# A decoder layer on one core: the merge by halves of the tokens, the first half inside the recurrent stage's stream of products

## The chip, the core and the metric

The kernel runs on one core of a Trainium2 chip. A core has five engines with a queue of instructions each: TensorE (PE, matrix products; its weight loads, PEld, overlap them), VectorE (DVE), ScalarE (ACT), GpSimd (POOL) and SyncE (SP). Each works through its own queue in order, and an instruction that waits holds up all that stand behind it on that engine. Products are summed in PSUM, eight banks of 128 x 512 float32; everything else lives in SBUF. DMAs are issued from the queues of SP, ACT and POOL. The metric is the time of one launch in microseconds (us) on the device; the median of the runs is what counts.

## What is computed

One decoder layer over 512 tokens of width 1024, in float32. Two branches run on the same normalised rows, attention (`y_a`) and a recurrence (`y_b`), are raised to full width, gated, added, and projected; a norm and a feed-forward part follow.

```python
y_a = _diff_branch(p_q, p_k, p_v, ...)
y_b = _rwkv_branch(p_rwkv, ...)          # a scan over the 512 tokens
merged = (jax.nn.sigmoid(p_ga) * (y_a @ w_up_a[l])
          + jax.nn.sigmoid(p_gb) * (y_b @ w_up_b[l]))
mix = merged @ w_out[l]
h = _layer_norm(DEEPNORM_ALPHA * h + mix, ln1_g[l], ln1_b[l])
ffn = (jax.nn.silu(h @ ffn_w_gate[l]) * (h @ ffn_w_up[l])) @ ffn_w_down[l]
h = _layer_norm(DEEPNORM_ALPHA * h + ffn, ln2_g[l], ln2_b[l])
```

`w_up_b` is 512 x 1024, `w_out` 1024 x 1024, the feed-forward width 2816.

## The kernel before

Every large product is done in split precision: a float32 operand is held as a rounded part (h) and a remainder (l), and `three` (L79) issues three matmuls, h·h, h·l and l·h. A piece of weights is 128 x 1024 floats (512 KB). SP loads it into one of two buffers `w_raw`, ACT casts it to h (L75), DVE subtracts to get l (L76), and both land in rotating tiles `w_h` and `w_l` (three of each). `split_psum` (L116) does the same for activations.

The kernel has three parts. First entry norm, attention, and the projections. Second the recurrent stage (L757 to L985), whose instructions are written out in an order that the program works out itself: generators yield the costs they expect on PE, DVE and ACT, and a small planner (L936 to L983) keeps a clock for each engine and takes the first task that is ready. The order of the list is the priority. Ahead stand the recurrence's steps: `chains`, `posts` (finishing of 128 tokens each: norm over heads, gain, gate), `applies`, `rwkv_solve`, `pres`, `mids`, and `yb_split`, which splits the finished `y_b` into h and l. Behind stand the fill tasks: `stream(gates)` and `ups`, the up-projection of `y_a`, both through `stream` (L787), which prefetches two pieces ahead. The list `fill` names them, for a rule that gives them a least share of PE. Each engine gets its instructions in that order; instructions of what follows the stage may be put between them by the framework where it finds an engine free.

Post `tb` ends with L655 to L661: for the first three blocks of 128 tokens y goes out to DRAM on POOL's queue (`y_d`) and `yb_split` loads it back; the last block stays in SBUF (`y_last`).

Third, L988 on: the merge. For each of four column groups j, `group_a` (L84) does the up-projection of `y_b` over all 512 tokens (24 matmuls of 512 columns); `gated` (L782) multiplies with the stored gate `thb`, DVE adds the attention branch's `tha`, ACT and DVE split the sum into `mg` (L1009 to L1012); then one piece of `w_out` serves the output products of columns 0 to 511 for all four blocks of 128 rows (L1014 to L1023). After that come the output products of columns 512 to 1023 (`out_proj`, L1038), block of rows by block of rows; each ends with the residual, the norm and a store of `h1`; `to_h2` (L1062) transposes a block of normalised rows into `h2`, the operand of the feed-forward products. The first gate and up group of the feed-forward part is done by halves of the tokens (L1100 to L1112), with `to_h2(2)` and `to_h2(3)` in its order. Outside the recurrent stage the framework orders instructions by their readiness and by place in the program.

## Time and profile before

| | us |
|---|---|
| median of 3 runs | 890.8 |
| the runs | 895.94, 890.8, 890.51 |
| the profiled execution | 890.32 |
| its span, first to last instruction | 888.6 |
| PE busy in the span | 834.4 |
| mean granted clock | 0.979 |

All working below is against the one profiled execution. A line of the profile that begins with a time is an instruction (or several like it) in order of time: start, duration, engine, line, operation, what it writes and reads, the shape, and in brackets how long the engine stood idle before it and what released it. A line that begins with a line number is a group: count, busy time and mean duration in ns of one, then idle time before. In the table of stretches each engine has its busy time and in brackets its instructions; the granted clock (1.00 is full speed) follows them. Two matmuls overlap, so their pace is the distance of their starts, not their duration.

### The profile page before, as it was taken

Reading aid. Unit: us, or ns where it says so; the run is one execution under the profiler, and the core shown is the slowest. Engines: PE = TensorE matmul, PEld = TensorE weight load, DVE = VectorE, ACT = ScalarE, POOL = GpSimd, SP = SyncE. Lnnn points to the kernel's source line nnn. Section 1 sums busy time; section 2 is a strip of 40 time slices with the busy share of each in tenths; the row PEclk is TensorE's granted clock in tenths of the full one; section 3 lists DMA queues with packets and bytes.
Section 4 is the critical chain, followed back from the end, with each engine's and each line's share of the span. In section 5 each row is a group of like instructions: output and inputs, shape, how many; then the busy total and the mean of one; then the engine's idle time right before and its main releaser. Section 6 shows DMA issues by size and latency. Waiting matters only on the chain. (4 is left out here: it accounts for less than half of the span.)

```text
span 888.6 us, 13458 instructions
## 1 busy us (share of the span) xinstructions
PE 834.4 (94%) x5486; PEld 684.7 (77%) x5486; DVE 457.2 (51%) x821; ACT 329.1 (37%) x572; POOL 82.5 (9%) x126
## 2 busy tenths in 40 slices
PE   3999999989799998988799999999999999999996
PEld 2877977878678776766577898888888888888885
DVE  6767494564648345636456954334434433324227
ACT  4566485736442344532124122222232223211210
POOL 5012010012230001201000100000000000000003
PEclk9999999998799999999799999999999999999999
DMA  6561422233234712134374444333333332222322
GB/s 224 152 215 53 127 60 83 72 96 72 54 90 142 169 48 96 61 107 155 101 268 141 142 178 137 105 102 96 95 94 95 95 95 95 95 96 71 120 71 96
DMA packets 75596, 99.15 MB, mean 112 GB/s; under 512 B 8431, under 2 KB 58154, under 8 KB 75534
## 3 DMA queue, kind: packets, MB, share of 16 engines
q1 hardware_dynamic: 70206, 80.72, 30.2%
q10 hardware_dynamic: 3488, 11.54, 3.5%
q0 software_dynamic: 1840, 6.03, 2.2%
q8 instruction: 43, 0.70, 0.3%
q14 instruction: 19, 0.16, 0.0%
HBM read 84.90 MB, written 14.69 MB: 112 GB/s over the span
## 5 line engine op out<-in xcount | busy, mean ns | idle before, releaser
L80 PE MATMUL mm_ps<-act_h,w_h 128*128 128x512 f32 x624 | 252.1, 404 | 1.0 <-ACT w_h L75 1.0
L82 PE MATMUL mm_ps<-act_h,w_l 128*128 128x512 f32 x624 | 245.7, 394 | 0.5 <-DVE w_l L76 0.5
L81 PE MATMUL mm_ps<-act_l,w_h 128*128 128x512 f32 x624 | 245.4, 393 | 0.0
L76 DVE TENSOR_TENSOR w_l<-w_raw,w_h 128x1024 fp32r<-128x1024 f32 x84 | 102.7, 1224 | 151.1 <-ACT w_h L75 150.9
L75 ACT CAST w_h<-w_raw 128x1024 fp32r<-128x1024 f32 x84 | 88.3, 1051 | 201.4 <-PE acc_ps L82 81.2
L82 PEld LDWEIGHTS mm_ps<-act_h,w_l 128*128 128x128 f32 x624 | 118.4, 190 | 25.3 <-DVE w_l L76 1.0
L80 PEld LDWEIGHTS mm_ps<-act_h,w_h 128*128 128x128 f32 x624 | 118.3, 190 | 25.1 <-ACT w_h L75 1.4
L81 PEld LDWEIGHTS mm_ps<-act_l,w_h 128*128 128x128 f32 x624 | 118.4, 190 | 21.7
L100 POOL TENSOR_TENSOR rs<-ve,mhalf 128x1 f32<-128x1 f32 (+1 forms) x32 | 29.4, 920 | 511.7 <-DVE ve L98 436.9
L82 PE MATMUL acc_ps<-w_h,hid_l 128*128 128x512 f32 (+1 forms) x198 | 73.4, 371 | 0.0
L81 PE MATMUL acc_ps<-w_l,hid_h 128*128 128x512 f32 (+1 forms) x198 | 73.3, 370 | 0.0
L80 PE MATMUL acc_ps<-w_h,hid_h 128*128 128x512 f32 (+1 forms) x198 | 73.2, 370 | 0.0
L804 DVE TENSOR_TENSOR w_l<-w_raw,w_h 128x1024 fp32r<-128x1024 f32 x32 | 39.0, 1222 | 37.1 <-ACT w_h L803 37.1
L80 PEld LDWEIGHTS acc_ps<-w_h,hid_h 128*128 128x128 f32 x198 | 37.3, 188 | 7.1
L82 PEld LDWEIGHTS acc_ps<-w_h,hid_l 128*128 128x128 f32 x198 | 37.3, 188 | 7.0
L81 PEld LDWEIGHTS acc_ps<-w_l,hid_h 128*128 128x128 f32 x198 | 37.2, 188 | 6.9
L803 ACT CAST w_h<-w_raw 128x1024 fp32r<-128x1024 f32 x32 | 33.4, 1047 | 16.2 <-PE mm_ps L81 13.8
L1092 ACT CAST hid_h<-sl 128x512 fp32r<-128x512 f32 x22 | 13.6, 617 | 54.0 <-DVE sl L1090 54.0
L1090 DVE SCALAR_TENSOR_TENSOR sl<-sl,mm_ps 128x512 f32<-128x512 f32 x20 | 13.8, 688 | 33.1 <-PE mm_ps L82 33.1
L1087 DVE SCALAR_TENSOR_TENSOR sl<-sl,mm_ps 128x512 f32<-128x512 f32 x20 | 13.7, 685 | 33.0 <-ACT sl L1086 33.0
L81 PE MATMUL acc_ps<-wo_l,mg_h 128*128 128x512 f32 x64 | 25.2, 394 | 2.1 <-DVE wo_l L1018 2.1
L1086 ACT ACTIVATE sl<-mm_ps 128x512 f32<-128x512 f32 x20 | 11.8, 592 | 39.9 <-PE mm_ps L82 39.9
(266 smaller groups left out, 1242.9 us busy)
## 6 DMA issues: line engine op xcount, KB each, us to landing
w_raw<-in_w_in SPq DMA_DIRECT2D x42, 512.0 KB
w_raw<-in_ffn_w_gate SPq DMA_DIRECT2D x22, 512.0 KB
w_raw<-in_ffn_w_up SPq DMA_DIRECT2D x22, 512.0 KB
w_raw<-in_ffn_w_down SPq DMA_DIRECT2D x22, 512.0 KB
w_raw<-in_w_out SPq DMA_DIRECT2D x8, 512.0 KB
hres_d<-xt POOLq DMA_DIRECT2D x4, 512.0 KB, 7.2
tha_d<-th ACTq DMA_DIRECT2D x4, 512.0 KB
thb_d<-th ACTq DMA_DIRECT2D x4, 512.0 KB
```

Of the source, the lines that this page charges most:

```text
L75: nc.scalar.copy(out=h, in_=raw)
L76: nc.vector.tensor_tensor(out=l, in0=raw, in1=h.bitcast(F32), op=ALU.subtract)
L80: nc.tensor.matmul(ps, wh, ah, start=first, stop=False)
L81: nc.tensor.matmul(ps, wh, al, start=False, stop=False)
L82: nc.tensor.matmul(ps, wl, ah, start=False, stop=last)
L100: nc.gpsimd.tensor_tensor(out=rs, in0=ve, in1=mhalf[:, 0:1].broadcast_to([P, n]), op=ALU.pow)
L803: nc.scalar.copy(out=h, in_=raws[i])
L804: nc.vector.tensor_tensor(out=l, in0=raws[i], in1=h.bitcast(F32), op=ALU.subtract)
L1086: nc.scalar.activation(out=sl[:, m, :], in_=ps, func=AF.Tanh, scale=0.5)
L1087: nc.vector.scalar_tensor_tensor(out=sl[:, m, :], in0=sl[:, m, :], scalar=1.0, in1=ps, op0=ALU.add, op1=ALU.mult)
L1090: nc.vector.scalar_tensor_tensor(out=sl[:, m, :], in0=sl[:, m, :], scalar=0.5, in1=ps, op0=ALU.mult, op1=ALU.mult)
L1092: nc.scalar.copy(out=h, in_=sl[:, m, :])
```

## The change

The merge is cut at token 256.

- Posts 0 and 1 no longer store y: they split it at once into `yb0` (tokens 0 to 255), in buffers with the tags of SC and AR. `yb_split` does the other half.
- A new fill task, `half_merge`, stands last in the list. It holds until `ups`, post 0 and post 1 are done. It issues six DMAs on POOL's queue (two of `hr`, 512 KB each, four of `thb`, 256 KB each) into the buffers that yh and yl had. Then it streams four up-projection groups over 256 tokens (24 matmuls of 256 columns each, `pe` cost scaled) and the output products of blocks 0 and 1, in two groups of four `w_out` pieces; `residual` with its statistics follows each finished block. `mg` now lives in the buffers of `act_h` and `act_l`.
- `merge(j)`, in the third part, does the other 256 tokens: up-projection, then two pieces of `w_out`, for both column halves. The norms of rows 0 to 255 (`norm_rows(0)`, `(1)`) stand between the merges, those of rows 256 to 511 behind `merge(3)`.
- Weights of `w_up_b` and `w_out` are thus loaded and split twice: 12 pieces more.
- Pools move: PSUM of the third part is `mps`, `h2` has a pool of its own, and the first eight of the 22 slices of `hid` lie in the `act` buffers.

```diff
-    def group_a(w, c0, nk, ah, al, evac, ncol=256):
+    def group_a(w, c0, nk, ah, al, evac, ncol=256, n=S):
...
-            ps = mm.tile([P, S], F32, name="mm_ps", tag="mm_ps")
+            ps = mm.tile([P, S], F32, name="mm_ps", tag="mm_ps")[:, 0:n]
...
-        if tb < NT4 - 1:
+        if tb < 2:
+
+            if "yb0" not in box:
+                box["yb0"] = [rk.tile([P, 4, 2 * TB], F32R, name=f"y{x}0", tag=t, bufs=NT4) for x, t in zip("hl", ("SC", "AR"))]
+            nc.vector.tensor_tensor(out=yt, in0=ps, in1=yt, op=ALU.mult)
+            split_psum(yt, *(x[:, :, ts] for x in box["yb0"]))
+            yield dict(pe=0.8, d=2.1, a=0.65)
+            return
+        if tb == 2:
...
         for g in groups:
+            if "wo" in g:
+
+                mg = g["x"]()
+                pss = [mm.tile([P, S], F32, name="mm_ps", tag="mm_ps") for _ in range(2)]
+                for q in range(4):
+                    for t in range(2):
+                        tq = slice(t * P, (t + 1) * P)
+                        for k in range(2):
+                            cost = split(i + 1) if t + k == 0 else {}
+                            h, l = parts[i]
+                            kk = 2 * q + k
+                            three(pss[t], mg[0][:, kk, tq], mg[1][:, kk, tq], h[:, k, :], l[:, k, :], kk == 0, kk == KD - 1)
+                            if kk == KD - 1:
+                                g["evac"](t, pss[t])
+                                cost = dict(g["cost"])
+                            yield dict(cost, pe=0.69)
+                    i += 1
+                continue
...
+    def to_mg(th, j, ts):
+        nc.vector.tensor_tensor(out=th, in0=th, in1=tha[j][:, :, ts], op=ALU.add)
+        mh, ml = (x[:, 2 * j:2 * j + 2, ts] for x in bx["mg"])
+        nc.scalar.mul(out=mh, in_=th, mul=0.5)
+        nc.vector.scalar_tensor_tensor(out=ml, in0=th, scalar=0.5, in1=mh.bitcast(F32), op0=ALU.mult, op1=ALU.subtract)
...
+    def half_merge():
+        while not (bx.get("ups") and bx.get("post0") and bx.get("post1")):
+            yield dict(hold=True)
+        hr = bx["gp"].tile([P, 2, D], F32, name="hr0", tag="yh")
+        for t in range(2):
+            nc.gpsimd.dma_start(out=hr[:, t, :], in_=hres_d[t * P:(t + 1) * P, :])
+        thb = bx["gp"].tile([P, 4, 2, H], F32, name="thb0", tag="yl")
+        for j in range(4):
+            nc.gpsimd.dma_start(out=thb[:, j], in_=th_d[1][j][:, :, 0:H])
...
+        def up_b(j):
+            return dict(w=I['w_up_b'][0], c0=256 * j, nk=4, n=H, x=lambda: bx["yb0"], begin=lambda: thb[:, j], evac=gated,
+                        end=lambda th: to_mg(th, j, slice(0, H)), cost=dict(d=0.9, a=0.3))
+
+        def wo_cols_of(n):
+            return dict(w=wo_cols, c0=512 * n, nk=KD, wo=True, x=lambda: bx["mg"],
+                        evac=lambda t, ps: residual(hr[:, t, :], t, n, ps), cost=dict(d=1.4))
+
+        yield from stream([up_b(j) for j in range(4)] + [wo_cols_of(n) for n in range(2)])
...
         tasks = [[t, 0.0] for t in (chains(), posts(0), posts(1), applies(), ya_split(), rwkv_solve(bx), pres(0), pres(1), mids(),
-                                    yb_split(), stream(gates), ups())]
-        fill = tasks[-2:]
+                                    yb_split(), stream(gates), ups(), half_merge())]
+        fill = tasks[-3:]
...
+    def merge(j):
+        th = ph2.tile([P, 2, H], F32, name="thb", bufs=2)
+        nc.sync.dma_start(out=th, in_=th_d[1][j][:, :, H:S])
+        group_a(I['w_up_b'][0], 256 * j, 4, yb[0], yb[1], lambda m, ps: gated(th, m, ps), n=H)
+        to_mg(th, j, slice(H, S))
+        ws = []
+        for n in range(2):
+            raw_w = wts.tile([P, 2, 512], F32, name="w_raw", tag="w_raw", bufs=2)
+            nc.sync.dma_start(out=raw_w, in_=wo[:, 2 * j:2 * j + 2, n * 512:(n + 1) * 512])
+            wh, wl = (ph2.tile([P, 2, 512], F32R, name=f"wo_{x}", bufs=3) for x in "hl")
+            nc.scalar.copy(out=wh, in_=raw_w)
+            nc.vector.tensor_tensor(out=wl, in0=raw_w, in1=wh.bitcast(F32), op=ALU.subtract)
+            ws.append((wh, wl))
+        for t in range(2):
+            ts = slice(H + t * P, H + (t + 1) * P)
+            for n, (wh, wl) in enumerate(ws):
+                for k in range(2):
+                    kk = 2 * j + k
+                    three(ps0[t][n], mg[0][:, kk, ts], mg[1][:, kk, ts], wh[:, k, :], wl[:, k, :], kk == 0, kk == KD - 1)
...
-    out_proj(0)
-    out_proj(1)
-    out_proj(2)
-    to_h2(0)
-    out_proj(3)
-    to_h2(1)
+    merge(0)
+    norm_rows(0)
+    merge(1)
+    norm_rows(1)
+    to_h2(0)
+    merge(2)
+    to_h2(1)
+    merge(3)
+    norm_rows(2)
+    norm_rows(3)
```

More of the change, by code (lines that the diff above doesn't have):

```diff
@@ L790, in stream @@
             wv = g["w"].rearrange("(k p) c -> p k c", p=P)
-            pieces += [wv[:, k0:k0 + 4, g["c0"]:g["c0"] + 256] for k0 in range(0, g["nk"], 4)]
+            if "wo" in g:
+                pieces += [wv[:, k0:k0 + 2, g["c0"]:g["c0"] + 512] for k0 in range(0, g["nk"], 2)]
+            else:
+                pieces += [wv[:, k0:k0 + 4, g["c0"]:g["c0"] + 256] for k0 in range(0, g["nk"], 4)]
         raws, parts = {}, {}
@@ L795, in load @@
             if i < len(pieces):
-                raws[i] = wts.tile([P, 4, 256], F32, name="w_raw", tag="w_raw", bufs=2)
+                raws[i] = wts.tile(list(pieces[i].shape), F32, name="w_raw", tag="w_raw", bufs=2)
                 nc.sync.dma_start(out=raws[i], in_=pieces[i])
@@ L800, in split @@
             if i < len(pieces) and i not in parts:
-                h = wts.tile([P, 4, 256], F32R, name="w_h", tag="w_h")
-                l = wts.tile([P, 4, 256], F32R, name="w_l", tag="w_l")
+                h = wts.tile(list(pieces[i].shape), F32R, name="w_h", tag="w_h")
+                l = wts.tile(list(pieces[i].shape), F32R, name="w_l", tag="w_l")
                 nc.scalar.copy(out=h, in_=raws[i])
@@ L915, in ups @@
         yield from stream([up_group(j) for j in range(4)])
-    def yb_split():
-        fs = []
-        for tb in range(NT4 - 1):
-            while not (bx.get(f"post{tb}") and "ya" in bx):
-                yield dict(hold=True)
-            fs.append(bx["gp"].tile([P, 4, TB], F32, name="yf", bufs=3))
-            nc.sync.dma_start(out=fs[tb], in_=y_d[1][:, :, tb * TB:(tb + 1) * TB])
-            yield dict(lat=4.0)
-        bx["yb"] = yb = [rv.tile([P, 4, S], F32R, name=f"yb_{x}", tag=f"raw_{n}") for x, n in zip("hl", "vk")]
-        for tb in range(NT4):
-            while tb == NT4 - 1 and "y_last" not in bx:
-                yield dict(hold=True)
-            f = bx["y_last"] if tb == NT4 - 1 else fs[tb]
-            split_psum(f, *(x[:, :, tb * TB:(tb + 1) * TB] for x in yb))
+        bx["ups"] = True
@@ new lines, in layer, with residual @@
+    H = 2 * TB
+    wo_cols = I['w_out'][0]
+    sts = [small.tile([P, 2, 6], F32, name=f"sts{t}", bufs=1) for t in range(4)]
+    def to_mg(th, j, ts):
[3 more added lines that the diff above has]
+        nc.vector.scalar_tensor_tensor(out=ml, in0=th, scalar=0.5, in1=mh.bitcast(F32), op0=ALU.mult, op1=ALU.subtract)
+    def residual(z, t, n, ps):
+        z = z[:, n * 512:(n + 1) * 512]
+        nc.vector.scalar_tensor_tensor(out=z, in0=z, scalar=ALPHA, in1=ps, op0=ALU.mult, op1=ALU.add)
+        nc.vector.bn_stats(out=sts[t][:, n, :], in_=z)
@@ new lines, in yb_split @@
+    def yb_split():
+        while not (bx.get("post2") and ("mid", NT4 - 1) in bx and "ya" in bx):
+            yield dict(hold=True)
+        f = bx["gp"].tile([P, 4, TB], F32, name="yf", bufs=3)
+        nc.sync.dma_start(out=f, in_=y_d[1][:, :, 2 * TB:3 * TB])
+        yield dict(lat=4.0)
+        bx["yb"] = yb = [rv.tile([P, 4, H], F32R, name=f"yb_{x}", tag=f"raw_{n}") for x, n in zip("hl", "vk")]
+        for tb in range(2):
+            while tb and "y_last" not in bx:
+                yield dict(hold=True)
+            split_psum(bx["y_last"] if tb else f, *(x[:, :, tb * TB:(tb + 1) * TB] for x in yb))
@@ L997, in layer @@
     nc.scalar.dma_start(out=b1, in_=I['ln1_b'].broadcast_to([P, D]))
[L998 to L1000 removed]
+    hrs = [bx["hr"][:, t, :] for t in range(2)]
+    for t in range(2, 4):
+        hr = ph2.tile([P, D], F32, name="hr", bufs=2)
         nc.scalar.dma_start(out=hr, in_=hres_d[t * P:(t + 1) * P, :])
         hrs.append(hr)
[L1003 to L1023 removed]
@@ L1044, in out_proj, with norm_rows @@
+    def norm_rows(t):
         hr = hrs[t]
-        residual(t, 1, ps)
+        if t >= 2:
+            for n in range(2):
+                residual(hr, t, n, ps0[t - 2][n])
         mv = small.tile([P, 2], F32, name="mv")
@@ L1054, in out_proj @@
             nc.vector.scalar_tensor_tensor(out=z, in0=z, scalar=rs, in1=b1[:, x * 512:(x + 1) * 512], op0=ALU.mult, op1=ALU.add)
[L1055 to L1060 removed]
+        nc.gpsimd.dma_start(out=h1_d[t * P:(t + 1) * P, :], in_=hr)
     def to_h2(t):
@@ L1099, in layer @@
         first.append([piece(wv[:, k0:k0 + 4, 0:256], 4, 256) for k0 in range(0, KD, 4)])
-    pss = [[acc.tile([P, S], F32, name="acc_ps", tag="acc_ps") for _ in range(2)] for _ in range(2)]
+    pss = [[mps.tile([P, S], F32, name="o_ps", bufs=4) for _ in range(2)] for _ in range(2)]
     for half in range(2):
@@ L1121, in layer, with hid @@
     nc.scalar.dma_start(out=b2, in_=I['ln2_b'].broadcast_to([P, D]))
-    hid = [fp.tile([P, KF, S], F32R, name=f"hid_{x}") for x in "hl"]
+    hid_a = [act.tile([P, KD, S], F32R, name=f"act_{x}", tag=f"act_{x}") for x in "hl"]
+    hid_b = [fp.tile([P, KF - KD, S], F32R, name=f"hid_{x}") for x in "hl"]
+    def hid(x, kk):
+        return hid_a[x][:, kk, :] if kk < KD else hid_b[x][:, kk - KD, :]
     res = []
```

75 lines of the change are left out of this document (19 added, 56 removed).

## The prediction

> **What bounds the kernel now.** Three views, in this order. First the page: the span, and the engine that is busy nearly all of it.
>
> ```profile
> span 888.6 us, 13458 instructions
> PE 834.4 (94%) x5486; PEld 684.7 (77%) x5486; DVE 457.2 (51%) x821; ACT 329.1 (37%) x572; POOL 82.5 (9%) x126
> ```
>
> TensorE (PE) is the bound, and the change leaves its arithmetic as it is: it can gain only where PE waits or runs slowly, and lose only where it makes PE wait. So second, busy time by stretches around the code that is edited: end of the recurrent stage, its tail, then the merge, the norms, the first FFN products. Columns: stretch, length, then busy us (instructions) of PE, weight loads, DVE, ACT, POOL, then granted clock, DMA share, GB/s.
>
> ```profile
> 410.00:430.50 20.50, 17.20 (x158) 13.53 (x156) 13.29 (x34) 6.89 (x12) 1.43 (x3) 0.92 0.39 128
> 430.50:439.10 8.60, 2.92 (x13) 2.20 (x12) 3.72 (x7) 2.12 (x5) 1.94 (x1) 0.70 0.01 2
> 439.10:452.50 13.40, 13.40 (x48) 10.82 (x49) 3.97 (x5) 2.94 (x3) 0.00 (x0) 0.81 0.84 310
> 452.50:485.00 32.50, 28.97 (x124) 22.86 (x124) 19.49 (x19) 9.35 (x9) 0.00 (x0) 1.00 0.58 180
> 485.00:514.50 29.50, 29.26 (x135) 23.49 (x133) 27.07 (x43) 6.91 (x9) 4.73 (x6) 1.00 0.37 118
> 514.50:540.00 25.50, 25.14 (x209) 24.94 (x210) 12.06 (x20) 7.39 (x11) 1.56 (x2) 1.00 0.55 194
> ```
>
> Third, what PE waited for from 410 to 545 us, and the rows of the order of time behind it.
>
> ```profile
> PE po_ps L624 <- DVE yt L657: 3.0, 1, 3.0
> PE po_ps L646 <- DVE y L641: 2.6, 1, 2.6
> PE acc_ps L81 <- DVE wo_l L1018: 2.1, 1, 2.1
> PE po_ps L655 <- ACT yt L648: 1.9, 2, 1.6
> PE mm_ps L80 <- ACT yb_h L117: 1.5, 1, 1.5
> PE acc_ps L80 <- ACT mg_h L1011: 1.0, 1, 1.0
> ...
> 430.33 0.39 PE L82 MATMUL mm_ps<-yh,w_l 128*128 128x512 f32 x1
> 430.42 2.02 POOL L100 TENSOR_TENSOR rs<-ve,mhalf 128x8 f32<-128x8 f32 x1 [10.33 <-DVE ve L98]
> 432.48 0.69 DVE L641 TENSOR_TENSOR y<-y,rs 128x512 f32<-128x512 f32 x1 [0.35 <-POOL rs L100]
> 433.32 0.63 PE L646 MATMUL po_ps<-ident,y 128*128 128x128 f32 x4 [2.60 <-DVE y L641]
> 439.10 1.22 PE L80 MATMUL mm_ps<-yb_h,w_h 128*128 128x512 f32 x2 [1.49 <-ACT yb_h L117]
> 440.12 0.63 PE L81 MATMUL mm_ps<-yb_l,w_h 128*128 128x512 f32 x1
> 440.55 0.63 PE L82 MATMUL mm_ps<-yb_h,w_l 128*128 128x512 f32 x1
> 445.00 0.39 PE L80 MATMUL mm_ps<-yb_h,w_h 128*128 128x512 f32 x1
> 449.58 0.39 PE L82 MATMUL mm_ps<-yb_h,w_l 128*128 128x512 f32 x1
> 519.99 0.28 PE L80 MATMUL acc_ps<-act_h,w_h 128*128 128x256 f32 x1
> 520.95 0.29 PE L82 MATMUL acc_ps<-act_h,w_l 128*128 128x256 f32 x1
> ```
>
> The fill of the recurrent stage (gates, then `ups`) ends at 430.33. The chain of the last 128 tokens ends later, and PE has 2.92 us of work in 8.60 us: 5.7 us idle. After that the granted clock is 0.81: two neighbouring matmuls start 0.43 us apart (440.12, 440.55), against 0.229 at full clock (445.00 and 449.58 are first and last of 21). Twelve or so such matmuls lose 2.4 us. So the tail costs 8.1 us. The merge adds 2.1 + 1.0 us of waits. That is all the change aims at, about 11 us of 890. From 485 to 514.5 DVE is busy 27.07 of 29.50 us: it is nearly the bound there.
>
> **The change, part by part.** Durations for the sum:
>
> ```profile
> L76 DVE TENSOR_TENSOR w_l<-w_raw,w_h 128x1024 fp32r<-128x1024 f32 x11 | 13.4, 1222 | 11.0 <-ACT w_h L75 11.0
> L75 ACT CAST w_h<-w_raw 128x1024 fp32r<-128x1024 f32 x11 | 11.6, 1051 | 29.3 <-DMA w_raw<-in_ffn_w_gate 8.1 <-PE mm_ps L81 7.3 <-DMA w_raw<-in_w_up_b 5.7
> L783 DVE SCALAR_TENSOR_TENSOR thb<-thb,mm_ps 128x512 f32<-128x512 f32 x8 | 5.4, 685 | 12.9 <-PE mm_ps L82 7.2 <-DMA thb<-thb_d 5.7
> L609 DVE TENSOR_TENSOR Sa<-e,Sa 128x256 f32<-128x256 f32 x1 | 0.4, 425 | 0.2 <-PE e L603 0.2
> L117 ACT CAST act_h<-acc_ps 128x512 fp32r<-128x512 f32 x8 | 4.4, 589 | 23.5 <-PE acc_ps L1068 23.5
> L118 DVE TENSOR_TENSOR act_l<-acc_ps,act_h 128x512 fp32r<-128x512 f32 x8 | 5.3, 671 | 3.8 <-ACT act_h L117 3.8
> L1060 DVE BATCH_NORM_STATS2 sts<-hr 128x6 f32<-128x512 f32 x8 | 5.4, 688 | 0.1
> L1051 DVE SCALAR_TENSOR_TENSOR hr<-hr,mv,g 128x512 f32<-128x512 f32 x8 | 5.6, 744 | 0.0
> L658 POOL DMA_DIRECT2D yb_d<-yt x1 | 0.7, 734 | 7.0 <-DVE yt L657 7.0
> yb_d<-yt POOLq DMA_DIRECT2D x1, 256.0 KB, 3.0
> 469.46 9.10 SPq L1030 DMA_DIRECT2D w_raw<-in_w_out  x4
> 416.88 1.22 DVE L76 TENSOR_TENSOR w_l<-w_raw,w_h 128x1024 fp32r<-128x1024 f32 x1
> 418.13 0.69 DVE L657 TENSOR_TENSOR yt<-po_ps,yt 128x512 f32<-128x512 f32 x1
> 523.87 1.29 DVE L118 TENSOR_TENSOR act_l<-acc_ps,act_h 128x512 fp32r<-128x512 f32 x2 [1.17 <-ACT act_h L117]
> ```
>
> (a) *Splits of y for tokens 0 to 255 move into posts 0 and 1*, and two loads leave SP's queue. Same DVE and ACT time; costed at nothing, since PE has the fill to run beside them. Also, at 416.88 a split of merge weights stood ahead of L657, for which PE waited; that weight now comes later. Gain 1.2 us.
>
> (b) *When the new fill starts.* `half_merge` is behind `ups` in the list and holds until `ups` is done: it stands behind 430.5, and so covers the tail, nothing earlier. Its `hr` and `thb` take the buffers of yh and yl, which the last `ups` matmul reads. They are six DMAs on POOL's queue, behind the power at L100 (430.42 + 2.02 = 432.4). Two of `hr` and one of `thb` at 0.73 us each give 434.6, plus 3.0 to land: 437.6. Earliest, with no wait behind L100: 430.7 + 2.2 + 3.0 = 435.9, or 435.3 with shorter issues. Latest, with the megabyte of `hr` ahead at the 310 GB/s of the row from 439.1 (3.4 us): 441. I take 437.5, as nothing else loads then. Until it lands, DVE stands in `gated`, with the last post's steps queued behind it; PE has both `mm_ps` banks full and can do one group, 24 matmuls of 256 columns at 0.12 us (519.99 to 520.95, eight steps), 2.9 us. So PE stands idle from 434.0 (430.5 + 2.9 + 0.63 of the post's transposes at 433.32) to 437.9, 3.9 us. Rows say what idle does here: after the bare tail the clock was 0.81 for 13.4 us, after the merge's waits of 2.1 and 1.0 us it stayed 1.00. I take the slow products after 437.9 as hidden, since DVE's period in (c) is longer than PE's. The Trainium skill ("TensorE: Matmul & The Clock Gate", HAM oscillation) speaks against the change here: an idle stretch of some 3.4 us, whatever its cause, puts the array back to half clock for the next window. The trace agrees for the tail (clock 0.70, then 0.81); by that rule, were nothing slower than PE after 437.9, an estimate of half a window, 1.7 us, would come on top: 897.5 instead of 895.8.
>
> (c) *The up-projection of the half.* Per group on DVE, in the written order: weight split 1.22, two `gated` on 256 columns 2 x 0.42, add 0.69, then ACT's mul 0.59 and its next weight cast 1.05 (DVE's 0.69 for the low part runs beside the cast), then the next split. 1.22 + 0.84 + 0.69 + 0.59 + 1.05 = 4.4 us against PE's 2.9. Three groups pass before the first split of w_out: 437.5 + 13.2, plus five DVE steps of the last post and of the remaining y splits (0.69 each, 3.5; bounds 0 and 3.5; I take 2.5, since L641 may come earlier): output products start at 453.2. By then PE has done half of the up-projection. Before, it had done as much (48 matmuls of 512) at 452.5. Net +0.7: the covered tail is handed back. Idle of 1.5 us per group should not lower the clock, as the 1.5 to 2.1 us waits of the merge did not (clock 1.00 from 452.5).
>
> (d) *Output products of the half*: eight pieces of w_out, 12 matmuls each, 2.74 us. SP's four issues take 9.10 us, three intervals of 3.0: the pace of two raw buffers. 8 x 0.3 = +2.1; nothing if casts run ahead.
>
> (e) *Second half, in the merge.* Per j now 24 x 0.12 + 24 x 0.229 = 8.4 us of PE, three pieces at 3.0 = 9.0. 4 x 9.0 = 36.0, against 144 matmuls x 0.229 = 33.0 for that share before. +3.0, less the 2.1 + 1.0 of waits that go with the old order: 0. Bounds -2.6 and +2.
>
> (f) *Norms of rows 256 to 511.* Formerly three blocks of output products covered them. Now both come after the last product: per row block two residuals (0.69, as L783), two statistics (0.69) and four passes (0.74): 5.7 us of DVE, 11.4 for both, with three first FFN weight splits (3.7) and four h2 splits (2.7): 17.8. Some 18 matmuls, 4.1 us, remain when the first sum is ready, so h2 is whole 13.7 us after the last product; PE has half of the first FFN products, 96 x 0.12 = 11.5. Exposed 2.2, or 3.4 with DVE's work stretched by its share of 0.92 (27.07 / 29.50), which I take. Bounds 0 and 7 (two pieces at 3.0 us ahead of the first product as well).
>
> Sum: -1.2 + 0.7 + 2.1 + 0 + 3.4 = +5.0. The profiled run took 890.3 us, 0.5 under the median; 895.3 on it, **895.8 us** as median. All low ends (T 435.3, no DVE steps of the post, d and e free, f at 0) give 883; all high ones 906. A check by DVE's own sum: 32.5 us in the half (4 x 3.44 + 8 x 1.22 + 4 x 1.37 + 3.45), 32.2 in the merge, 17.8 after it; 82.5 / 0.92 = 89.7, so from 437.5 h2 is whole at 527.2, against 525.2 before (523.87 + 1.29): +2.
>
> **The rivals.**
> *R1, faster.* Casts run ahead, so that (c) goes at PE's 2.9 us (-4.5), `thb` lands at 435.3 (-2.2), staging does not bind (-2.1, -2.6): 895.8 - 11.4 = 884, and 881 with norms hidden. It decides from a DVE period of 3 us on. For it: ACT is busy 9.35 of 32.5 us in the merge. Against: the order is written out, and cast follows mul.
> *R2, slower.* DVE becomes the bound: with in-order waits its share falls to 0.80 over the same 82.5 us: 103, h2 whole at 540.6, +15 at most; where PE's reserve takes a part, +9 to +12, near 902. It decides from a share under 0.85. For it: 19.49 of 32.5 us (0.60) in today's merge, when DVE waited for casts. Against: 0.92 when work was queued.
> *R3, no cover.* The last post is written out ahead of the new fill, so that the tail stays bare (8.1 us): T moves by some 5, 901. For it: L641, at 432.48, already stands right behind the last `ups` step. Against: its later steps are held by `lat` and ACT times.
>
> **How the numbers follow.** Forecast 0.45 (889 to 899.5), R1 0.20 (878 to 888), R2 0.25 (898 to 908), R3 0.10 (899 to 904). Range 884 to 906: two thirds of R1's lower part and the end of R2 lie outside, under 0.2. One per cent, about what a measurement can tell from no change, is 881.9 to 899.7: half of R1 is below it (0.10); R2 mostly and R3 mostly above (0.28); the rest, 0.62, within.
>
> **What would show it.** Right: `thb` landing at 436 to 440 with PE idle ahead of it; up-projection groups of the half 4 to 5 us apart; PE waits on w_l in the merge and on act_h or act_l in the first FFN half. Wrong: PE busy throughout 430 to 455 (R1), PE idle with DVE full after 500 for over 8 us (R2), 8 us still bare at the tail (R3). Wrong altogether, if the chain before 430 moves by more than 2 us, since I hold it fixed.

## The result, and the profile after

The changed kernel is slower: median 923.7 us (919.7 to 925.5, four runs) against 890.9 us, ratio 1.035 (95% interval 1.031 to 1.039). A second set gave 919.9 against 890.4, ratio 1.032 (1.030 to 1.034). The forecast was 895.8 us with a range of 884 to 906. All stage times below are from profiled executions: 925.1 us (span 923.3) for the changed kernel, 890.3 us (span 888.6) for the one before, a difference of 34.7 us.

The page of the changed kernel, the first lines:

```profile
span 923.3 us, 13760 instructions
PE 850.3 (92%) x5582; PEld 694.2 (75%) x5582; DVE 474.8 (51%) x849; ACT 342.0 (37%) x588; POOL 85.2 (9%) x130
PEclk9999999999999799999889999999999999999998
```

PE's share fell from 94 to 92%, but its busy time rose by 16 us although its arithmetic is the same. So about half of the loss is waiting, and half is products that run slower. The busy time by stretches, cut at the landmarks of this run (columns as in the prediction's table; the last three are the granted clock, the DMA share and GB/s):

```profile
410.00:432.90 22.90, 20.66 (x203) 16.21 (x202) 13.49 (x36) 5.01 (x12) 3.38 (x3) 1.00 0.25 77
432.90:461.70 28.80, 17.76 (x111) 16.60 (x109) 16.94 (x27) 9.03 (x13) 6.00 (x7) 0.82 0.49 162
461.70:493.60 31.90, 25.49 (x97) 18.86 (x97) 14.56 (x17) 8.92 (x9) 0.00 (x0) 0.89 0.64 212
493.60:542.90 49.30, 40.01 (x208) 33.71 (x209) 35.70 (x53) 18.95 (x22) 3.19 (x4) 0.93 0.56 178
542.90:569.30 26.40, 25.47 (x210) 24.40 (x209) 16.35 (x27) 6.37 (x10) 3.12 (x4) 1.00 0.59 208
569.30:793.30 224.00, 224.00 (x963) 179.94 (x962) 89.80 (x101) 65.00 (x82) 0.00 (x0) 1.00 0.33 97
```

From 432.9 to 542.9, the half and the second half of the merge, PE is idle for 26.7 of 110 us and the clock is below 1. Then nothing is idle, and yet the last row is the surprise: 224.0 us in which PE never waits, where the kernel before took 217.6. Here are the same landmarks in the runs that the text compares by stages, in us. The first column is the time at which the last product of `ups` starts; the others are lengths, from there to the start of the first output product of the merge; to the last output product; to the first feed-forward product of j=1; to the first down product; to the end of the span. (Up to the first output product PE has done the same work in all of these, 96 up-projection matmuls of 256 columns or 48 of 512; in the one with spare pieces only 24 of 512, so there the sum of the second and third stage is to be compared.)

| | last of `ups` | to output products | output products | to FFN j=1 | FFN | down, end |
|---|---|---|---|---|---|---|
| before | 430.3 | 22.2 | 60.4 | 27.0 | 217.6 | 131.0 |
| changed | 432.9 | 28.8 | 81.0 | 26.6 | 224.0 | 130.0 |
| changed, control | 429.9 | 25.8 | 79.4 | 26.5 | 224.0 | 130.1 |
| order left free | 429.2 | 18.9 | 75.3 | 26.4 | 224.0 | 130.1 |
| before, 12 spare pieces | 430.5 | 30.3 | 80.2 | 27.0 | 217.6 | 131.2 |
| loads moved | 430.8 | 24.0 | 75.3 | 26.7 | 228.1 | 130.1 |
| merge staged once | 436.9 | 27.4 | 70.0 | 25.4 | 224.0 | 130.1 |
| half staged once | 430.6 | 22.6 | 65.1 | 27.3 | 224.0 | 130.2 |
| spacer 2016 B | 433.6 | 27.8 | 80.6 | 26.7 | 217.6 | 128.3 |
| both staged once, spacer | 428.9 | 22.3 | 65.1 | 25.8 | 217.6 | 128.9 |
| before, spacer 224 B | 431.3 | 22.4 | 60.3 | 27.0 | 217.6 | 128.3 |

Changed less before: 2.6 + 6.5 + 20.6 - 0.4 + 6.4 - 1.0 = 34.7 us. Three entries carry it: the 6.5, the 20.6 and the 6.4. What PE waited for between 430 and 545 us, in the changed kernel (total, times, longest):

```profile
PE mm_ps L80 <- DVE thb L791: 7.6, 3, 4.8
PE mm_ps L80 <- ACT w_h L814: 6.4, 2, 4.5
PE o_ps L80 <- issue: 3.5, 1, 3.5
PE o_ps L80 <- ACT act_h L956: 2.9, 1, 2.9
PE mm_ps L80 <- ACT w_h L75: 1.7, 1, 1.7
```

And the order of time behind the first two (the profile leaves buffer numbers out, so `yb0` stands here as yh and yl, and `mg`, which lies in the buffers of `act`, as act_h and act_l):

```profile
433.31 2.03 POOL L100 TENSOR_TENSOR rs<-ve,mhalf 128x8 f32<-128x8 f32 x1 [8.97 <-DVE ve L98]
435.30 1.18 POOL L969 DMA_DIRECT2D hr<-hres_d  x2
436.45 2.86 POOL L972 DMA_DIRECT2D thb<-thb_d  x4
437.22 1.50 SPq L808 DMA_DIRECT2D w_raw<-in_w_up_b  x2
...
442.45 0.75 DVE L791 SCALAR_TENSOR_TENSOR thb<-thb,mm_ps 128x256 f32<-128x256 f32 x2 [4.12 <-DMA thb<-thb_d]
446.10 1.05 ACT L814 CAST w_h<-w_raw 128x1024 fp32r<-128x1024 f32 x1 [1.50 <-DMA w_raw<-in_w_up_b]
447.18 1.23 DVE L815 TENSOR_TENSOR w_l<-w_raw,w_h 128x1024 fp32r<-128x1024 f32 x1 [1.86 <-ACT w_h L814]
448.32 0.68 DVE L651 TENSOR_TENSOR yt<-yt,bon 128x512 f32<-128x512 f32 x1
449.11 0.69 DVE L668 TENSOR_TENSOR yt<-po_ps,yt 128x512 f32<-128x512 f32 x1
450.54 0.69 DVE L118 TENSOR_TENSOR yb_l<-yt,yb_h 128x512 fp32r<-128x512 f32 x1 [0.74 <-ACT yb_h L117]
451.15 0.74 DVE L791 SCALAR_TENSOR_TENSOR thb<-thb,mm_ps 128x256 f32<-128x256 f32 x2
451.71 0.55 PE L80 MATMUL mm_ps<-yh,w_h 128*128 128x256 f32 x1 [4.76 <-DVE thb L791]
452.06 0.42 PE L81 MATMUL mm_ps<-yl,w_h 128*128 128x256 f32 x1
452.27 0.42 PE L82 MATMUL mm_ps<-yh,w_l 128*128 128x256 f32 x1
455.39 0.41 DVE L791 SCALAR_TENSOR_TENSOR thb<-thb,mm_ps 128x256 f32<-128x256 f32 x1
...
461.40 4.47 SPq L808 DMA_DIRECT2D w_raw<-in_w_out  x2
471.72 1.04 ACT L814 CAST w_h<-w_raw 128x1024 fp32r<-128x1024 f32 x1 [7.51 <-DMA w_raw<-in_w_out]
472.81 0.80 PE L80 MATMUL mm_ps<-w_h,act_h 128*128 128x512 f32 x1 [4.50 <-ACT w_h L814]
```

`thb` is usable at 442.45. The piece of `w_up_b` that SP issued at 437.2 beside these 2 MB is cast only at 446.10, nine us later. DVE splits it, does three waiting steps of the last post, and comes to `gated` at 451.15; PE has stood with both banks full since 446.9. Another piece, issued at 461.40 beside the loads of g1, b1, hr and thb, is cast at 471.72: 10.3 us. After the first of these gaps products start 0.21 us apart (452.06, 452.27) instead of 0.12.

### The profile page after: what moved, and what is told of

Read it like the earlier page. It is cut to its first block, busy times and chain, and to the rows that moved or that the text cites. A ratio compares the mean times of both kernels' runs of the same rounds, so it can differ in the third digit from the quotient of the medians.

```text
span 923.3 us, 13760 instructions
## 1 busy us (share of the span) xinstructions
PE 850.3 (92%) x5582; PEld 694.2 (75%) x5582; DVE 474.8 (51%) x849; ACT 342.0 (37%) x588; POOL 85.2 (9%) x130
## 5 line engine op out<-in xcount | busy, mean ns | idle before, releaser
L80 PE MATMUL mm_ps<-act_h,w_h 128*128 128x512 f32 x304 | 128.1, 422 | 1.4 <-ACT w_h L75 1.4
L81 PE MATMUL mm_ps<-h_l,w_h 128*128 128x512 f32 x320 | 126.4, 395 | 0.0
L82 PE MATMUL mm_ps<-h_h,w_l 128*128 128x512 f32 x320 | 126.4, 395 | 0.0
L80 PE MATMUL mm_ps<-h_h,w_h 128*128 128x512 f32 x320 | 126.4, 395 | 0.0
L82 PE MATMUL mm_ps<-act_h,w_l 128*128 128x512 f32 x304 | 122.2, 402 | 0.5 <-DVE w_l L76 0.5
L81 PE MATMUL mm_ps<-act_l,w_h 128*128 128x512 f32 x304 | 121.8, 401 | 0.0
L100 POOL TENSOR_TENSOR rs<-ve,mhalf 128x1 f32<-128x1 f32 (+1 forms) x32 | 29.8, 931 | 539.7 <-DVE ve L98 531.6
L81 PEld LDWEIGHTS mm_ps<-h_l,w_h 128*128 128x128 f32 x320 | 60.0, 187 | 14.7
L80 PEld LDWEIGHTS mm_ps<-h_h,w_h 128*128 128x128 f32 x320 | 60.0, 187 | 14.6
L82 PEld LDWEIGHTS mm_ps<-h_h,w_l 128*128 128x128 f32 x320 | 60.0, 187 | 14.6
L80 PEld LDWEIGHTS mm_ps<-act_h,w_h 128*128 128x128 f32 x304 | 58.5, 193 | 13.4 <-ACT w_h L75 1.8
```

The source lines that it names most:

```text
L80: nc.tensor.matmul(ps, wh, ah, start=first, stop=False)
L81: nc.tensor.matmul(ps, wh, al, start=False, stop=False)
L82: nc.tensor.matmul(ps, wl, ah, start=False, stop=last)
L100: nc.gpsimd.tensor_tensor(out=rs, in0=ve, in1=mhalf[:, 0:1].broadcast_to([P, n]), op=ALU.pow)
```

## The experiments

Three theories, as they stood before the first runs: A, that late loads make the gaps; B, that the written order does, with other tasks' steps between the half's own; C, that twice the weight pieces through two raw buffers are the bound.

**The order left free.** `half_merge` leaves the planner's list and is issued after it, so that the framework orders it.

```diff
-    yb_split(), stream(gates), ups(), half_merge())]
-    fill = tasks[-3:]
+    yb_split(), stream(gates), ups())]
+    fill = tasks[-2:]
 ...
+    for _ in half_merge():
+        pass
     work.close()
```

> The changed kernel with the work of tokens 0-255 (half_merge) given out only after the last step of the stream, so that no step of the last position blocks stands between its instructions; the same instructions, loads and raw buffers otherwise. Theory A (late loads: the 2 MB of hr and thb at 433-442 us, and the later burst of g1, b1, hr and thb, stretch the weight pieces, and two raw buffers cannot cover it): the gaps on TensorE of 5.0 and 4.5 us stay, 923.7 us within +-5 (919 to 929). Theory B (the written order: VectorE and ScalarE steps of the last posts stand between the half's casts, evacuations and merges, so that a group takes 4.4 us and more instead of TensorE's 2.9): the gaps go and the time falls by 10 us or more, to 900-914. Theory C (twelve more pieces through two raw buffers are themselves the bound): no change, 923.7 within +-5, and the pieces come at the same pace of 3.5 us.

911.8 us, ratio 1.025 (1.020 to 1.030): in theory B's range, outside that of A and C. The changed kernel is at 1.035 and, in its control, at 1.032, so the written order is worth 6 to 9 us, a quarter of the loss. The stretch from the last product of `ups` to the output products, in this profile:

```profile
429.20:448.00 18.80, 15.17 (x110) 14.40 (x109) 12.98 (x21) 7.99 (x12) 5.50 (x7) 0.91 0.55 196
```

18.9 us in the table against 22.2 before: the bare tail is covered here, by 3.3 us, and of the waits on `thb` and `w_h` none is over 2.0 us. What the change wants does exist; the output products behind it (75.3 us against 60.4) give it back four times over.

**Spare pieces in the kernel before.** Nothing is moved; 12 more pieces are loaded and split in its merge, and not used.

```diff
+        for _ in range(spare):
+            piece(wv[:, 0:4, c0:c0 + ncol], 4, ncol)
 ...
-        raw_w = wts.tile([P, 2, 512], F32, name="w_raw", tag="w_raw", bufs=2)
+        for _ in range(3):
+            raw_w = wts.tile([P, 2, 512], F32, name="w_raw", tag="w_raw", bufs=2)
```

> The kernel before with nothing moved, but in its merge every w_up_b piece is loaded and split twice and every w_out piece of columns 0-511 three times (12 more pieces of 512 KB through the two raw buffers, the copies unused). Theory C (staging through two raw buffers is the bound once the pieces are doubled): the merge takes 12 times about 3 us longer less what its products hid, so +12 to +30 us: 903-921 us. Theory A (pieces cost little unless another burst of loads runs beside them): the merge's 33 us hold 24 pieces at about 1.5 us of transfer each, so +0 to +6 us: 891-897. Theory B expects under +6 us too, since no position block's step stands in the merge. An added 12 ScalarE casts (about 0.9 us each) and 12 VectorE subtractions (about 1.2 us each) are in both figures.

916.1 us, ratio 1.030 (1.026 to 1.034): +27 us. Theory C's range held it; A and B, which expected under 6, are wrong on this point. The round of one raw buffer, in the order of time, between the first and the last of 22 casts (two pieces had been cast earlier):

```profile
451.79 1.98 ACT L1020 CAST wo_h<-w_raw 128x1024 fp32r<-128x1024 f32 x2
...
463.22 6.94 SPq L1018 DMA_DIRECT2D w_raw<-in_w_out  x3
467.46 1.05 ACT L1020 CAST wo_h<-w_raw 128x1024 fp32r<-128x1024 f32 x1 [1.09 <-DMA w_raw<-in_w_out]
468.54 1.23 DVE L1021 TENSOR_TENSOR wo_l<-w_raw,wo_h 128x1024 fp32r<-128x1024 f32 x1 [0.92 <-ACT wo_h L1020]
...
519.04 1.05 ACT L1036 CAST wo_h<-w_raw 128x1024 fp32r<-128x1024 f32 x1 [2.60 <-DMA w_raw<-in_w_out]
```

A buffer is taken by a load at 463.22, cast when it has landed (467.46), subtracted (468.54 to 469.77), and only then free: 6.5 us a round. With two buffers that is some 3.2 us a piece, and (519.04 - 451.79) / 21 = 3.2 on the whole. In the changed kernel the casts of the 24 pieces of half and merge, from 434.09 to 531.96, come 4.26 us apart; these are the first and the last of them:

```profile
434.09 1.04 ACT L814 CAST w_h<-w_raw 128x1024 fp32r<-128x1024 f32 x1 [3.58 <-DMA w_raw<-in_w_up_b]
...
531.96 1.05 ACT L1084 CAST wo_h<-w_raw 128x1024 fp32r<-128x1024 f32 x1 [5.22 <-PE o_ps L82]
```

The products of one piece are worth 2.75 us of PE. With 12 pieces for 66 us of products staging had slack to hide its late pieces; with 24 it has none, and a late piece has nothing to hide behind. The round alone does not give the whole loss, though: 24 x (3.2 - 2.75) is some 11 us, an estimate from these rows, and the two stages lost 27.1. Why the pieces came 4.26 us apart (4.05 in the control) and not 3.2, no run takes apart.

**The loads moved.** `thb` first on POOL's queue, `hr` when the output products begin, g1, b1 and the other `hr` behind the half's last cast.

```diff
+        def wo_begin(n):
+            for t in range(0 if n else 2):
+                nc.gpsimd.dma_start(out=hr[:, t, :], in_=hres_d[t * P:(t + 1) * P, :])
 ...
+    with tc.issue_after(bx["cast"].ins):
+        nc.scalar.dma_start(out=g1, in_=I['ln1_g'].broadcast_to([P, D]))
```

> The changed kernel with its loads put elsewhere and nothing else: on POOL's queue thb goes first and the two hr rows only when the half's output products begin; g1, b1 and hr of rows 256-511 on ScalarE's queue are issued only behind the half's last weight cast. Theory A: thb[0] lands about 2-4 us earlier, the piece that took 9 us lands in 3-5, the gaps of 5.0 and 4.5 us shrink to under 2 us each and the half clock behind them goes with them: 8 to 16 us less, 908-916 us. Theories B and C: the gaps move to the next in-order step or the next piece, under 4 us less, 920-926.

920.7 us, ratio 1.038 (1.033 to 1.044): no gain, as B and C had it, and the 8 to 16 us of theory A did not come. Its profile is of the fastest of its four runs (916.7 us; the slowest took 927.3). There the way from `ups` to the first FFN product of j=1 is 5.6 us shorter than in the control. A cast of its merge stands 7.1 us for its load, behind the burst that the half had escaped, and 4.1 us come back in the FFN stage, where a product waits 2.2 us for the split of a weight piece and 3.4 us at half clock follow. So moving the loads moved the waits; that they cost nothing where they stood is not shown.

**Only the up-projection joins.** The output products, residuals and norms stay as before; four pieces are doubled. Against the kernel before:

```diff
+        yield from stream([up_b(j) for j in range(4)])
 ...
-        th = ph2.tile([P, 2, S], F32, name="thb", bufs=2)
-        nc.sync.dma_start(out=th, in_=th_d[1][j])
-        group_a(I['w_up_b'][0], 256 * j, 4, yb[0], yb[1], lambda m, ps: gated(th, m, ps))
+        th = ph2.tile([P, 2, H], F32, name="thb", bufs=2)
+        nc.sync.dma_start(out=th, in_=th_d[1][j][:, :, H:S])
+        group_a(I['w_up_b'][0], 256 * j, 4, yb[0], yb[1], lambda m, ps: gated(th, m, ps), n=H)
```

> Only the up-projection of tokens 0-255 joins the stream; the output projection, the residuals and the norms stay whole in the merge as in the kernel before (4 more w_up_b pieces, no w_out piece doubled, no hr on POOL's queue). By the landmarks of the changed kernel the up-projection of the half alone is 7.3 us late, 2.6 of them already there when it begins; the output products and the second half give the other 25. Theory A: without hr in front and without the 8 doubled w_out pieces some 0 to +8 us against the kernel before, 891-899. Theory B: the half's groups still stand in the written order, +5 to +10, 896-901. Theory C: 4 doubled pieces of 12, a third of the loss of 33 us, +8 to +14, 899-905. If the product's cover is real, and none of the three holds here, it is faster than before by 3 to 8 us, 883-888: the halved period of the merge's first part.

907.1 us, ratio 1.021 (1.017 to 1.024), beyond all three ranges. Its profile is 15.9 us longer than the kernel before: 10.6 up to the first FFN product of j=1, and 6.4 in the FFN stage (224.0 against 217.6), less 1.1 after it. In the FFN stage the products read two tiles, the weights and `h2`, and of these `h2` lies in a pool of its own, as in the changed kernel. None of the theories had that. It opened the next question.

**The place of `h2`.** The FFN products have no idle time in either kernel. Products in 100 us, the kernel before first, then the changed one (the first number in brackets counts the matmuls):

```profile
600.00:700.00 100.00, 100.00 (x443) 82.79 (x442) 41.23 (x47) 29.60 (x37) 0.00 (x0) 1.00 0.33 95
```

```profile
600.00:700.00 100.00, 100.00 (x431) 80.31 (x430) 39.50 (x45) 28.94 (x36) 0.00 (x0) 1.00 0.33 95
```

443 against 431 at full clock; the starts are 226.7 and 233.3 ns apart. Shape, type and count are the same, only the tile differs. In the built programs `act`, `w_h` and `w_l` begin at 1952 past a multiple of 2048 bytes (160 past one of 256), the new `h2` at 1984 (192 past one of 256). So a spacer was put in front.

```diff
     h2p = ctx.enter_context(tc.tile_pool(name="h2p", bufs=1))
+    h2p.tile([P, 8], F32, name="spacer")
     h2 = [h2p.tile([P, KD, S], F32R, name=f"h2_{x}") for x in "hl"]
```

> The changed kernel itself, run again as the control of the three beside it: 923.7 within +-4 us. In its first profile the granted clock was 0.5 for 13.7 us from 300 us on, in code that the change does not touch; the kernels with the same code up to there had 0, 3.4 and 10.2 us of it. If that is chance, this profile shows another length again; if the change causes it, 13.7 us again.

> The changed kernel with a spacer of 32 bytes per partition ahead of h2 in its pool; nothing else differs but the SBUF addresses of h2, hid and the tiles behind them. The first FFN products (h2 against w_h and w_l, 512 columns) start 233.4 ns apart in the changed kernel and 226.7 ns apart in the kernel before, where h2 lay in the act tiles; the stage of 960 products takes 224.0 us instead of 217.6. Theory P (the pace depends on the address: act and w_h begin 32 bytes past a multiple of 64, h2 and hid of the changed kernel on one, and operands that lie differently to 64 bytes cost 16 cycles a product): 226.7 ns again, and with hid's products too some 6 to 9 us less than the changed kernel beside it. Theory Q (it depends on the distance in SBUF, or on which pool, not on 32 bytes): 233.4 ns as before, no difference within +-4 us.

The control took 919.9 us (ratio 1.032), the spacer of 32 bytes 918.4 (1.031, 1.029 to 1.033): the same within the intervals, so the 6 to 9 us did not come. But the pace moved, from 233.3 to 228.9 ns, and the FFN stage from 224.0 to 219.8 us. Neither theory said that.

The same spacer of 32 bytes went ahead of `hid` in the kernel before, whose down products have `hid` as the stationary operand and start 233 ns apart.

> The kernel before with the same spacer of 32 bytes ahead of hid alone. Its down-projection products (hid as the stationary operand, w_h and w_l as the moving one) start 230 to 236 ns apart, those of its first FFN stage 226.7. Theory P: 227 ns in the down-projection too, 594 products times 6 ns: 2 to 4 us faster than the kernel before, ratio 0.996 to 0.998. Theory Q: ratio 1.000 within its interval. A version faster than both kernels, if P holds.

890.5 us, ratio 1.000 (0.997 to 1.002), and 233.2 ns still: theory P, with its 64 bytes, is wrong. What remained was that fast pairs agree in a longer remainder. In the changed kernel the spacer was made 2016 bytes (504 floats).

> The changed kernel with a spacer of 2016 bytes ahead of h2, so that h2 and hid begin at 1952 past a multiple of 2048 bytes, as act, w_h and w_l do. Theory R: the 960 products of h2 start 226.7 ns apart instead of 233.3, and those of hid 227 instead of 233.2 (378 of them): 6 to 9 us less than the changed kernel, 912-915. Theory Q: 233.3 ns, no difference within +-3 us.

912.6 us, ratio 1.023 (1.018 to 1.028), and 226.7 ns: theory R holds, and 217.6 us for the FFN stage. Which remainder counts was asked of three profiles, of one run each, with spacers of 96, 224 and 480 bytes (24, 56 and 120 floats):

> The changed kernel with 96 bytes ahead of h2, so that h2 agrees with act and w_h in its remainder to 128 bytes, but not to 256. Only the pace is asked, from the profile: 226.7 ns a product of h2 if 128 bytes are what counts, 229 to 233 if more do.

> The same with 224 bytes: h2 agrees with act and w_h to 256 bytes, but not to 512. 226.7 ns a product of h2 if 128 or 256 bytes are what counts, 229 to 233 if more do.

> The same with 480 bytes: h2 agrees with act and w_h to 512 bytes, but not to 1024. 226.7 ns a product of h2 if 512 bytes or fewer are what counts, 229 to 233 if 1024 or 2048 do.

First 96 bytes, then 224:

```profile
600.00:700.00 100.00, 100.00 (x432) 81.10 (x431) 39.18 (x44) 28.88 (x36) 0.00 (x0) 1.00 0.30 95
```

```profile
600.00:700.00 100.00, 100.00 (x443) 82.81 (x442) 41.34 (x47) 29.74 (x37) 0.00 (x0) 1.00 0.31 95
```

232.4 ns with 96 bytes, 226.7 with 224 and with 480. It is the remainder to 256 bytes. The three runs took 925.0, 916.3 and 914.3 us.

In all of these the fast pairs begin at 160 past a multiple of 256, so they do not tell whether the two operands must agree or must both lie at 160. The kernel before tells it, in its merge, where neither lies at 160. The stationary operand `mg` begins at 192 past a multiple of 256. The `wo` pieces of columns 0 to 511 begin at 192 too, those of the other columns at 224. Products of the two kinds follow each other without a wait at 493.19, and full clock is granted to both:

```profile
490.00:493.20 3.20, 3.20 (x16) 2.63 (x15) 2.95 (x5) 1.05 (x1) 0.00 (x0) 1.00 0.84 253
493.20:506.40 13.20, 13.20 (x58) 10.64 (x57) 12.77 (x22) 1.05 (x1) 2.60 (x3) 1.00 0.38 122
```

The 15 products from 490.02 to 492.96 start 226.7 ns apart, the 58 from 493.19 to 506.49 233.3. So it is the agreement that counts, and 32 bytes between the operands cost what they cost with `h2`.

**The kernel before, with `hid` moved by 224 bytes.** It takes theory R to the other kernel, and was planned together with the 2016 bytes, before the remainder to 256 was known.

```diff
     fp = ctx.enter_context(tc.tile_pool(name="fp", bufs=1))
+    fp.tile([P, 56], F32, name="spacer")
     g2 = fp.tile([P, D], F32, name="g2")
```

> The kernel before with a spacer of 224 bytes ahead of hid, so that hid begins at 1952 past a multiple of 2048 bytes, as act, w_h and w_l do (32 bytes, which gave 1760, changed nothing: 233.2 ns a down-projection product before and after). Theory R (products run at 227 ns when stationary and moving operand have the same remainder, at 233 otherwise; the 32 bytes ahead of h2 changed 233.3 to 228.9): 227 ns in the down-projection, 594 products by 6 ns, 3 to 4 us faster, ratio 0.995 to 0.997. Theory Q (distance in SBUF, or hid as the stationary operand): 233.2 ns, ratio 1.000.

887.1 us against 891.1, ratio 0.995 (0.993 to 0.998): faster than both kernels, from a spacer alone. 100 us of its down projection, the kernel before first:

```profile
760.00:860.00 100.00, 100.00 (x472) 82.54 (x471) 27.03 (x28) 18.92 (x18) 0.00 (x0) 1.00 0.29 95
```

```profile
760.00:860.00 100.00, 100.00 (x482) 84.40 (x481) 29.09 (x29) 19.17 (x19) 0.00 (x0) 1.00 0.29 99
```

**More raw buffers in the merge.**

```diff
-            raw_w = wts.tile([P, 2, 512], F32, name="w_raw", tag="w_raw", bufs=2)
+            raw_w = ph2.tile([P, 2, 512], F32, name="raw_w", bufs=2)
```

> The changed kernel whose merge of tokens 256-511 loads its w_out pieces into two raw buffers of their own, so that it has four raw buffers instead of two; the half in the stream keeps two. Casts of the merge's twelve pieces came 3.8 us apart in the changed kernel (490.5 to 532.0 us). Theory C (two raw buffers, each held for load, cast and subtraction, some 6 us a round): the twelve come 2.8 to 3.2 us apart, where TensorE's own 2.8 us bounds them, and the merge's 46.5 us fall to 35-40: 6 to 11 us less than the control. Theory B (the chain in written order, products to gated to sum to act_h to output products, 3 to 4 us bare for each group): no more than 2 us less, and the waits of the output products on the cast of act_h stay.

915.2 us, ratio 1.027 (1.023 to 1.031), about 4.5 us under the control: between the two theories, and the intervals of the two ratios leave anything from nothing to some 9 us, so it decides for neither. In its profile the second half of the merge takes 41.4 us (49.3 in the changed kernel, 50.2 in the control), but the output products of the half 33.9 (31.9 and 29.6); the early loads of the new buffers now run beside the half's own.

**Staging taken away.** Two kernels load and split only the first pieces of the merge, or of the half, and use them for all groups, so that the later groups multiply by the first group's weights; all products, evacuations and sums stay.

```diff
-        ws = []
-        for n in range(2):
+        ws = bx.setdefault("w2", [])
+        for n in range(0 if ws else 2):
```

```diff
+        def rep(i):
+            return min(i, 4) // 4 * 4 if once else i
 ...
+            if i < len(pieces) and rep(i) != i:
+                parts[i] = parts[rep(i)]
+                load(i + 2)
+                return {}
```

> The changed kernel, but the merge of tokens 256-511 loads and splits its three weight pieces for j=0 only and uses them for all four j (9 of 12 pieces left out, so the products of j=1 to 3 have the wrong weights; every product, evacuation and sum of the merge stays). 15 pieces in all, against 12 in the kernel before. Theory C (the doubled staging costs, as the 12 spare pieces in the kernel before did, 2.3 us a piece): 9 pieces less are 15 to 25 us less than the changed kernel, 895-905, and the merge's 46 to 50 us fall to 34-38. Theory B (the in-order chains: products, gated, sum, cast of act_h, output products): under 5 us less, 915-920; the merge stays above 43 us.

> The counterpart: the half in the stream loads and splits one w_up_b piece and one w_out piece and uses them for all its groups (10 of 12 pieces left out, wrong weights for tokens 0-255 but for the first pieces; all products, evacuations and sums stay), the merge keeps its 12. Theory C: 10 pieces at about 2.3 us: 18 to 27 us less, 893-902; the half's output products take their 22 us instead of 30 to 32, and the gaps of 5.0 and 4.9 us on TensorE go. Theory B: the groups of the up-projection stay at 4.4 us, and only the output products' waits on casts go: 4 to 10 us less, 910-916. If both this and the merge's counterpart give under 10 us each, neither staging alone carries the loss.

Merge: 912.0 us, ratio 1.023 (1.019 to 1.026), 8 us less than the control, so C was too high and B too low. Half: 902.4 us, ratio 1.013 (1.010 to 1.015), 17 us less, just past C's range. Stretches of the half's kernel, `ups` to output products, the half's, the merge:

```profile
430.60:453.20 22.60, 15.37 (x110) 14.17 (x109) 12.49 (x21) 6.25 (x11) 5.33 (x7) 0.92 0.35 123
453.20:480.50 27.30, 23.50 (x96) 19.04 (x97) 11.21 (x14) 4.82 (x5) 0.00 (x0) 0.94 0.60 207
480.50:518.50 38.00, 36.16 (x209) 31.26 (x208) 29.90 (x48) 13.63 (x17) 3.19 (x4) 1.00 0.47 150
```

The first stretch is back at the 22 us of the kernel before. The merge, whose 12 pieces are all still loaded, falls from 49 to 38 us: its pieces can now be fetched while the half's products run. That fits staging as one queue, in which a piece less at the head is time at the end.

**Both taken away, and the spacer.**

The three edits together.

> The changed kernel with both found costs taken away at once: the half and the merge each load and split the first pieces only (5 pieces instead of 24, wrong weights for the other groups) and the 2016-byte spacer stands ahead of h2. By the ratios of the runs so far the parts are worth 1.0319-1.0126 (half), 1.0319-1.0228 (merge) and 1.0319-1.0233 (addresses): if they add, 1.0319 less 0.0370 is 0.995, some 886 us, so that the cover by the joined products was worth a few us and staging and addresses account for all of the loss. If something third costs (written order, norms at the end), the ratio stays above 1.01, over 900 us.

893.9 us, ratio 1.004 (1.000 to 1.007): neither 0.995 nor above 1.01. Against the half alone that is 0.009 less, and the spacer alone was worth 0.0086. So the merge's 8 us do not come again: the output products take 65.1 us with and without the merge's staging. The two staging costs are one cost, some 17 us by the ratios. What staged once takes away is load, cast and subtraction together; which of them counts, these runs do not say.

## Why the prediction was wrong

The ratio of the control, 1.032, is 28.4 us on 890. By ratios: staging 17.2 (half staged once), addresses 8.0 (in the profile 6.4 in the FFN stage and 1.8 in the down projection), and 3.2 that remain with both gone. That these add up to 28.4 is no test, since each is the difference to the next run; the test is that the 8.0 agrees with the 7.7 of the spacer alone (1.0319 - 1.0233). Each ratio is known to 2 to 4 us. In the profile of that last kernel the output products still take 4.7 us more than before, with one wait of 4.0 us on the residual (`hr`), which stands in the half staged once too (3.8) and not in the kernel before; the end is 2.1 us shorter for `hid`. The order left free, 6 us, overlaps with the staging, and how much was not measured.

- *(a)* held: PE waits 2.0 us at the last post's first product instead of 3.0.
- *(b)* T was put at 437.5 with 441 as latest; it was 442.45, of which 2.9 came with a late L100 (433.31 for 430.42), and the rest is the time behind it, 9.1 for 7.1 us. "Nothing else loads then" was false: SP's two weight pieces were issued at 437.2 beside the 2 MB. The slow products that I took "as hidden" were not: the granted clock was 0.82, 0.89 and 0.93 in the three stretches up to 542.9, which is 28.8 x 0.36 + 31.9 x 0.22 + 49.3 x 0.14 = 24 us at half speed against 10 before (8.6 x 0.60 + 13.4 x 0.38). The extra 14 us cost at most 7, if they were full of products. The Trainium skill ("TensorE: Matmul & The Clock Gate", HAM oscillation) says that an idle window of about 3.4 us brings half clock for what follows; the trace agrees, with PE waits of 4.76 and 4.50 us and 0.82 and 0.89.
- *(c)* the net of +0.7 was +6.5, beside the 2.6 already there at the end of `ups`. The chain itself was sized about right: the second group, from `gated` at 451.15 to the next at 455.39, takes 4.24 us for my 4.4 (the third 5.7, with 1.4 of waiting for PE). Two things were not. `thb` is usable 9.5 us behind the last product of `ups`, where I had 7.0. From there the output products begin after 19.2 us, where I had 15.7: the first group takes 8.7 us (442.45 to 451.15), of which a cast waits 1.5 us for its load, a term that I put at nothing, and three steps of the last post take 2.8 (I had allowed 2.5 for five). The stretch falls to 22.6 with the half's pieces staged once, but that takes the load and the chain's own casts and splits away together; and it falls to 18.9 with the order left free and every piece loaded. So load and written order both enter, and no run here parts them.
- *(d)* and *(e)* are the step that failed. Eight pieces at 3.0 us (+2.1, which is 8 x (3.0 - 2.74); the 8 x 0.3 written there would be 2.4) and 36.0 less the old waits (0) took the distance of three issues in the old merge, 3.0 us, as the pace of doubled staging, and compared it with PE's time for the same products as if it were the only thing that could hold them up. Measured: the half's output products take 31.9 us for 22.0 of PE (+9.9), the rest 49.1 where the same share took 38.4 (+10.7), +20.6 for my +2.1. Three us is about what two raw buffers give when little is late (3.2 with the spare pieces). Against 2.75 us of products that leaves no slack, and the pace became 4.26. Staged once in the half, the two steps together cost +4.7 instead of +20.6. How the loss is shared between the round of the buffers, late loads and the written order stays open.
- *(f)* +3.4 was -0.4: the norms of rows 256 to 511 are covered by the first FFN products after all.
- *No step* had the 6.4 us of the FFN stage. The prediction ended where `h2` is whole and took everything behind as equal; the diff moves `h2` to another pool, and that was read as bookkeeping.
- *The chain before 430* moved by 2.6 us, more than the 2 that were given as a bound. In code that the change leaves alone, the clock was halved for 13.7 us from 300 us on, which costs 6.8 us at most. The kernel before, the changed kernel, and its control, in that stretch:

```profile
297.00:317.00 20.00, 18.46 (x305) 14.66 (x303) 5.44 (x8) 7.51 (x14) 0.62 (x1) 1.00 0.76 172
```

```profile
297.00:317.00 20.00, 17.94 (x193) 14.21 (x192) 4.72 (x6) 4.97 (x8) 0.61 (x1) 0.66 0.47 96
```

```profile
297.00:317.00 20.00, 18.38 (x311) 14.38 (x312) 6.17 (x10) 7.60 (x15) 0.62 (x1) 0.91 0.57 126
```

The control, the same program, has 3.4 us of it, and its last product of `ups` starts at 429.9; the kernel before with the 224-byte spacer has 10.2. So the change does not cause it, and it can set single runs of one kernel a few us apart.

Of the rivals, R2 had the sign and something of the condition (DVE's share falls to 0.72 in the merge, under its 0.85), but not the mechanism: DVE waits for casts and loads, and is not the bound. R1's premise, casts that run ahead, is the reverse of what happened. R3's delay of `thb` came, 5 us, but not its reason: the last post's steps stand between those of the new fill, and the loads were late.

## What to carry to other kernels

Halving the rows that a weight piece serves doubles the pieces, and what has to be compared is the round of a raw buffer (load, cast, subtraction: 6.5 us here) against the products of one piece: with 3.2 us a piece against 2.75 there is no slack, and adding spare pieces to the old kernel is a run that tells this before anything is rebuilt. When a tile moves to another pool, compare the pace of the products that read it, stage by stage, also where no engine waits. Two findings whose parts do not add up should be taken away together once, since that is how one sees that they are the same cost.
